# One root chain for both halves of a head slab and for two DeltaNet output tiles, and the identity kept inside the DeltaNet factor

## The chip, the core and the metric

The kernel runs on one core of a Trainium2 chip. Five engines work side by side on it: TensorE (PE, with its weight loads shown apart as PEld), VectorE (DVE), ScalarE (ACT), GpSimd (POOL) and SyncE (SP), which issues the DMAs. The metric is the device time of one execution in microseconds (us), and lower is better.

## The reference, cut to what matters

One layer of a decoder trunk on 512 tokens of width 1024. A normed input is projected once; its columns feed a gated DeltaNet (six heads of 64), a sparse attention (six query heads, two key/value heads) and a causal pooling. Their outputs are joined, projected back and added to the input, and a squared-ReLU MLP of width 4096 follows.

```python
def rms_norm(x, g):
    return xf * lax.rsqrt(jnp.mean(xf * xf, axis=-1, keepdims=True) + EPS) * g

# gated delta rule, chunks of 64 tokens
L = jnp.where(strict, einsum('bhncd,bhnsd->bhncs', k_beta, k) * decay, 0.0)
A = jnp.eye(C) + L
u = triangular_solve(A, v * beta, lower=True, unit_diagonal=True)
w = triangular_solve(A, k_beta * jnp.exp(gc), lower=True, unit_diagonal=True)
...
# DeltaNet output, per head
o = rms_norm(o, norm_g) * jax.nn.silu(z)
# attention: q, ks, kw are rms-normed per head of 64
q = rms_norm(q.reshape(B, T, NSA_HEADS, Dh), q_norm)
ks = rms_norm(ks, k_norm[1]); kw = rms_norm(kw, k_norm[2])
```

## The kernel before, in words

Tokens lie on the partitions in four tiles of 128 (`NT` = 4). The program runs in stages that flow into one another: input norm and first projections (to about 40 us), projection slabs for the DeltaNet with their convolutions (to about 120 us), the remaining slabs side by side with the DeltaNet solves and scan (to about 240 us), attention and output projection (to about 395 us), and the MLP (the rest).

**Order.** `side_by_side` (L935) merges five tracks into one program text: `solves`, `preps`, `slabs`, `compress` and `scans`. The context is opened with `schedule_with_timeline_sim=True`, so the order on each engine is fixed when the program is built, from the dependences and an estimate of durations; the program text sets priorities. At run time each engine works through its own list in that order.

**Root chain.** `rsqrt` (L101) finds a reciprocal root on DVE: a shift (L103), a multiply-add on the bits (L104) and three rounds of three small operations (L110, L111, L112). The caller puts one scaling ahead of it (L533 or L920) and sometimes one behind it (L536).

**Head slabs.** `prep_heads` (L521) norms the heads of one slab and transposes them. It is called three times: with four query heads that lie in `zt`, with a slab of two query and two key heads, and with a slab of two key heads; the latter two come out of `proj_tok` (L416), whose products lie in two PSUM banks `pss[0]` and `pss[1]`, one for token tiles 0 and 1, one for 2 and 3. For each half `b`: Square on ACT (L531, the first write of a buffer `qks`), sum on DVE (L532), scaling and root chain, product with the root (L537, the last read of `src[b]`), product with the norm weights on POOL (L540), then per tile a copy on ACT (L544, the first write of a buffer `X`) and a remainder on POOL (L545). The transposes (L549) and copies into `XT` (L552, L556, L557) follow when all four `X` are there. `qks`, `X`, `XT`, `Vt` and others share one pool of 27 buffers, `r2` (`t2`, L80). The banks of `pm` (L68) are 0, 1 and 2, so that of two successive slabs of `proj_tok` the second needs one bank of the first.

**DeltaNet.** `gdn_prep_k` (L747) makes the factor `LT` of a tile and its negative in fp16, `L16` (L767). `gdn_solve` (L812) builds an approximate inverse in fp16 and refines it with two calls of `residual` (L841): `IX` = I - `X` on DVE (L842), twelve-pair products of `LT` and `X` on PE (`sysmm`, L794), and `IX` minus them (L844). Four solves run, in two pairs side by side. `gdn_step` (L867) is the scan, nine steps long; its PSUM bank is number 3.

**DeltaNet output.** `gdn_out(i)` (L912) takes tile `i` when the scan has written it: Square (L918), sum (L919), scaling (L920) and root chain, product (L922), product with the gate on POOL (L923), three transposes into bank 3 (L926) and three pairs of copies out of it (`split_rows`, L147 to L149, into `yTh`, `yTl`). The four calls share bank 3 one after the other. Attention takes its accumulators from banks 7 and 3 (`pa`, L1054), so that its second head (`acc`, L1160) needs bank 3 after all four calls.

Of the kernel before, what the change touches and what calls it, by code (L numbers as in the profile page):

```python
# [9 lines left out]
F32 = mybir.dt.float32  # L10
# [27 lines left out]
def trunk_kernel(ctx, tc, x, norm_mix, w_in, conv_w, a_log, dt_bias, gdn_norm, nsa_q_norm, nsa_k_norm,  # L38
# [14 lines left out]
    def nm(s):  # L53
        _n[0] += 1
        return f"{s}{_n[0]}"
# [24 lines left out]
    def t2(shape, name, dt=F32):  # L80
        return r2.tile(shape, dt, tag="t", name=nm(name), bufs=N2)
# [19 lines left out]
    def rsqrt(y, a, n, p=P):  # L101

        V.tensor_single_scalar(y.bitcast(I32), a.bitcast(I32), 1, ALU.logical_shift_right)  # L103
        V.tensor_scalar(y.bitcast(I32), y.bitcast(I32), -1.0, float(0x5EF759DF - 0x80000000), ALU.mult, ALU.add)  # L104
        t = sml.tile([P, n], F32, tag=f"rs{n}", name=nm("rs"))[:p]
        for _ in range(3):
            if n == 1:
                V.scalar_tensor_tensor(t, y, a, y, ALU.mult, ALU.mult)
            else:
                V.tensor_tensor(t, y, y, ALU.mult)  # L110
                V.tensor_tensor(t, t, a, ALU.mult)  # L111
            V.scalar_tensor_tensor(y, t, -1.5, y, ALU.add, ALU.mult)  # L112
# [408 lines left out]
    def prep_heads(src, kg, qn, dst):  # L521


        n = len(dst)
        X = [t2([P, 4, P], "X") for _ in range(NT)]
        for b in range(2):
            scr = t2([P, 2, 4, HD], "qks")
            s_ = scr[:, :, 0:n]
            ss = sml.tile([P, 2, n], F32, tag=f"ssp{n}", name=nm("ss"))
            r = sml.tile([P, 2, n], F32, tag=f"rp{n}", name=nm("r"))  # L530
            S.activation(s_, src[b], AF.Square)  # L531
            V.tensor_reduce(ss, s_, AX.X, ALU.add)  # L532
            V.tensor_scalar(ss, ss, 0.5 / HD, 0.5 * EPS, ALU.mult, ALU.add)  # L533
            rsqrt(r.rearrange("p i h -> p (i h)"), ss.rearrange("p i h -> p (i h)"), 2 * n)
            if qn:
                V.tensor_scalar(r[:, :, 0:qn], r[:, :, 0:qn], 0.125, None, ALU.mult)  # L536
            V.tensor_tensor(s_, src[b], r.unsqueeze(3).to_broadcast([P, 2, n, HD]), ALU.mult)  # L537
            if qn < n:
                for i in range(2):
                    G.tensor_tensor(s_[:, i, qn:n], s_[:, i, qn:n],  # L540
                                    gk_b[:, kg].unsqueeze(1).to_broadcast([P, n - qn, HD]), ALU.mult)
            for i in range(2):
                x_ = X[2 * b + i]
                S.copy(x_[:, 0:n, 0:HD].bitcast(F32R), s_[:, i])  # L544
                G.tensor_tensor(x_[:, 0:n, HD:P], s_[:, i], x_[:, 0:n, 0:HD], ALU.subtract)  # L545
        for h, x0 in enumerate(dst):
            ps = pn()
            for i in range(NT):
                PE.transpose(ps[:, ts(i, P)], X[i][:, h, :], ident)  # L549
            XT[x0] = t2([P, T], "XT", F32R)  # L550
            if h < qn:
                S.copy(XT[x0], ps)  # L552
            else:
                XT[x0 + 1] = t2([P, T], "XT", F32R)
                for c in range(2):
                    S.copy(XT[x0 + c][halves[c]], ps[halves[c]])  # L556
                    V.tensor_copy(XT[x0 + c][halves[1 - c]], ps[halves[c]])  # L557
        return 0.43 * n
# [147 lines left out]
    gt = gte.enter_context(pool("gt", 1))  # L706
    GB = dict(kT=2, D1=2, LT=4, QK=4, qdT=4, tmp=3, gls=2, vn=2, S=3, L16=4)
    for a in range(2):
        GB.update({f"X{a}": 1, f"IX{a}": 1, f"TT1{a}": 1, f"T{a}": 4, f"R{a}": 2})

    def bch(r):
        return r.unsqueeze(2).to_broadcast([P, H, HD])

    def bs(m):
        return m.unsqueeze(1).to_broadcast([P, 6, 64])
# [31 lines left out]
    def gdn_prep_k(i):  # L747

        gU = w1t([P, 2, 3, 64], "gU", "tmp")
        gi = g[:, i].rearrange("p (j a) -> p a j", a=2)  # L750
        for hp in range(2):
            G.tensor_tensor(gU[:, hp], gi[:, hp].unsqueeze(2).to_broadcast([P, 3, 64]),
                            le64.unsqueeze(1).to_broadcast([P, 3, 64]), ALU.mult)
        de = pp_()
        PE.matmul(de[:, 0:384], sgt, gU.rearrange("p a j c -> p (a j c)"), start=True, stop=False, skip_group_check=True)
        PE.matmul(de[:, 0:384], identb, bs(nm64), start=False, stop=True, skip_group_check=True)
        yield 0.9
        D1, LT = w1t([P, 6, 64], "D1"), w1t([P, 6, 64], "LT")
        D0 = w1t([P, 6, 64], "D0", "tmp")
        S.activation(D1, v6(de), AF.Exp)  # L760
        V.tensor_tensor(D0, D1, bs(lt64), ALU.mult)
        kT = w1t([P, 3, 2, 64], "kT")
        S.copy(kT, head_T(kr[:, i]))
        yield 0.4
        yield from decayed(LT, kT, kT, D0)
        L16 = w1t([P, 6, 64], "L16", "L16", F16)
        V.tensor_scalar(L16, LT, -1.0, None, ALU.mult)  # L767
        grp[i] = dict(kT=kT, D1=D1, LT=LT, L16=L16)
        have.add(("k", i))

# [23 lines left out]
    def sysmm(pb, lhsT, rhs):  # L794

        ps = pb()
        for s_ in range(6):
            for p in range(2):
                PE.matmul(ps[halves[p], ts(s_, 64)], lhsT(halves[p], s_), rhs(halves[p], s_), start=True, stop=True)  # L799
        return v6(ps)  # L800

    def at(t):
        return lambda h, s_: t[h, s_]
# [8 lines left out]
    def gdn_solve(i):  # L812
# [7 lines left out]
        def tl(name, tag, dt=F32):  # L820
            return w1t([P, 6, 64], name, f"{tag}{ln}", dt)
# [14 lines left out]
                T16, TT16 = nt, tt  # L836
                yield 0.33

        X, IX = tl("X", "X"), tl("IX", "IX")

        def residual():  # L841
            V.tensor_tensor(IX, bs(id2), X, ALU.subtract)  # L842
            r = tl("R", "R", F16)
            V.tensor_tensor(r, IX, sysmm(pb, lambda h, s_: LT[h, s_], at(X)), ALU.subtract)  # L844
            return r

        G.tensor_copy(X, T16)
# [61 lines left out]
        yield 0.4  # L909
        return Sn  # L910

    def gdn_out(i):  # L912

        o = vb[:, i]
        sq = w1t([P, H, HD], "sq", "tmp")
        ss = sml.tile([P, H], F32, tag="ss6", name=nm("ss"))
        r = sml.tile([P, H], F32, tag="r6", name=nm("r"))
        S.activation(sq, o, AF.Square)  # L918
        V.tensor_reduce(ss, sq, AX.X, ALU.add)  # L919
        V.tensor_scalar(ss, ss, 0.5 / HD, 0.5 * EPS, ALU.mult, ALU.add)  # L920
        rsqrt(r, ss, 6)
        V.tensor_tensor(o, o, bch(r), ALU.mult)  # L922
        G.tensor_tensor(o, o, zt[:, i], ALU.mult)  # L923
        ps = go()
        for j in range(3):
            PE.transpose(ps[:, ts(j, P)], o[:, 2 * j:2 * j + 2].rearrange("p a d -> p (a d)"), ident)  # L926
        for j in range(3):
            split_rows(yTh[j][:, ts(i, P)], yTl[j][:, ts(i, P)], ps[:, ts(j, P)])


    def now(gen):
# [103 lines left out]
    slabs2 = late[-1]  # L1035
    flat = []
    side_by_side((90, solves()), (100, preps()), (102.0, slabs()), (10, compress()), (80, scans()))
    for i in range(NT):
        gdn_out(i)
    rgt0.close()  # L1040
    gte.close()
# [375 lines left out]
```

## Time and profile before

| what | value |
|---|---|
| median of 3 runs | 723.83 us (723.25 to 725.51) |
| the profiled execution | 724.29 us |
| its span | 722.50 us (1.79 us lie around it) |
| busy PE, DVE, ACT, POOL | 696.9, 554.8, 386.4, 170.6 us |
| granted TensorE clock | 0.995 of full speed |

A row of the timeline gives start and duration in us, engine, line, operation, output<-input, shape and count; what stands in brackets is the idle time of the engine just ahead of it and what ended that. A matmul's busy time runs to its modelled end, so successive matmuls overlap in it.

### The profile page before, as it was taken

What the parts mean: (1) busy time and instruction counts of PE and PEld (TensorE: products, weight loads), DVE (VectorE), ACT (ScalarE), POOL (GpSimd) and SP (SyncE); (2) the same over time, 40 slices, a digit from 0 to 9 for tenths busy, and PEclk for the clock granted to TensorE, in tenths of its full rate; (3) what the DMA queues carried; (4) which work ended last, traced back from release to release, by engine and by line L of the source; (5) the groups of instructions that cost most, each with busy time, mean ns of one, the idle gap of its engine ahead of it and who ended that gap; (6) DMA issues with size and microseconds to landing.
All of it is one profiled execution on the core that took longest, in us unless ns stands there. A gap on an engine that the chain in (4) does not pass through costs nothing.

```text
span 722.5 us, 13307 instructions
## 1 busy us (share of the span) xinstructions
PE 696.9 (96%) x5155; PEld 573.0 (79%) x5155; DVE 554.8 (77%) x1061; ACT 386.4 (53%) x768; POOL 170.6 (24%) x257
## 2 busy tenths in 40 slices
PE   8999999999999998999899999999999999999997
PEld 7888887888988776776579878888888888888885
DVE  5688998878686788877555997987968686886836
ACT  5455835565754558568633944444454544544430
POOL 5730004222123310000030330405032050504123
PEclk9999999999999999999999999999999999999999
DMA  6343223132410602222020153324051333311103
GB/s 222 92 108 102 73 60 88 32 96 61 129 31 4 234 1 59 88 88 89 1 87 2 59 176 117 116 84 131 20 174 59 121 112 117 117 55 65 56 0 116
DMA packets 49922, 62.20 MB, mean 86 GB/s; under 512 B 5494, under 2 KB 42564, under 8 KB 49860
## 3 DMA queue, kind: packets, MB, share of 16 engines
q1 hardware_dynamic: 48996, 61.16, 27.0%
q8 instruction: 40, 0.66, 0.4%
q10 hardware_dynamic: 864, 0.20, 0.1%
q14 instruction: 22, 0.18, 0.1%
HBM read 59.25 MB, written 2.10 MB: 85 GB/s over the span
## 4 chain that ended last, share of the span: by engine, by line
PE 71%; DVE 16%; ACT 4%; DMA 4%; issue 3%; POOL 1%; SPq 0%; DVEq 0%; ACTq 0%; POOLq 0%
PE ps L143 17%; PE ps L144 17%; PE ps L145 17%; PE ps L424 5%; PE ps L799 2%; PE ps L1139 2%; PE ps L1125 1%; DMA raw<-in_w_in_dram 1%; PE ps L587 1%; DVE lw L135 1%; DMA raw<-in_w_ffn_dram 1%; DMA x<-in_x_dram 1%; PE ps L1100 1%; DVE bl L1293 1%; DVE lwo L135 1%
## 5 line engine op out<-in xcount | busy, mean ns | idle before, releaser
L144 PE MATMUL ps<-h2l,hw 128*128 128x512 f32 (+1 forms) x280 | 105.1, 376 | 0.1
L145 PE MATMUL ps<-h2h,lw 128*128 128x512 f32 (+1 forms) x280 | 104.8, 375 | 0.0
L143 PE MATMUL ps<-h2h,hw 128*128 128x512 f32 (+1 forms) x280 | 104.0, 374 | 0.0
L1300 POOL TENSOR_TENSOR al<-gF,ah 128x512 fp32r<-128x512 f32 x24 | 36.2, 1508 | 225.4 <-ACT ah L1299 185.8
L143 PE MATMUL ps<-bh,ah 128*128 128x512 f32 x224 | 88.5, 395 | 0.7 <-DVE x L1386 0.7
L144 PE MATMUL ps<-bl,ah 128*128 128x512 f32 x224 | 88.1, 394 | 0.0
L145 PE MATMUL ps<-bh,al 128*128 128x512 f32 x224 | 84.6, 393 | 0.0
L1386 DVE TENSOR_TENSOR x<-ps,x 128x512 f32<-128x512 f32 x112 | 72.9, 681 | 10.6 <-PE ps L145 10.5
L1293 DVE TENSOR_TENSOR bl<-w2r,bh 128x1024 fp32r<-128x1024 f32 x40 | 57.8, 1447 | 6.8 <-ACT bh L1292 6.8
L144 PEld LDWEIGHTS ps<-h2l,hw 128*128 128x128 f32 x280 | 52.6, 188 | 10.4 <-DVE h2l L1264 0.3
L145 PEld LDWEIGHTS ps<-h2h,lw 128*128 128x128 f32 x280 | 52.6, 188 | 9.9
L143 PEld LDWEIGHTS ps<-h2h,hw 128*128 128x128 f32 x280 | 52.3, 188 | 10.2
L1300 POOL TENSOR_TENSOR al<-gS,ah 128x512 fp32r<-128x512 f32 x32 | 53.9, 1700 | 21.0 <-ACT ah L1299 21.0
L1292 ACT CAST bh<-w2r 128x1024 fp32r<-128x1024 f32 x40 | 41.8, 1047 | 28.9 <-PE ps L145 28.1
L135 DVE TENSOR_TENSOR lo<-raw,hi 128x512 fp32r<-128x512 f32 (+1 forms) x76 | 42.5, 582 | 13.8 <-ACT hi L134 11.2
L134 ACT CAST hi<-raw 128x512 fp32r<-128x512 f32 (+1 forms) x76 | 37.1, 519 | 28.6 <-DMA raw<-in_w_in_dram 7.6
L143 PEld LDWEIGHTS ps<-bh,ah 128*128 128x128 f32 x224 | 42.1, 188 | 11.4 <-ACT ah L1299 0.9
L145 PEld LDWEIGHTS ps<-bh,al 128*128 128x128 f32 x224 | 42.1, 188 | 9.7
L144 PEld LDWEIGHTS ps<-bl,ah 128*128 128x128 f32 x224 | 42.2, 188 | 9.5
L134 ACT CAST hw<-raw 128x1024 fp32r<-128x1024 f32 x32 | 32.1, 1046 | 26.2 <-PE ps L144 23.1
L135 DVE TENSOR_TENSOR lw<-raw,hw 128x1024 fp32r<-128x1024 f32 x32 | 40.1, 1287 | 5.3 <-ACT hw L134 5.3
L1299 ACT CAST ah<-gS 128x512 fp32r<-128x512 f32 x32 | 19.8, 621 | 45.1 <-DVE gS L1368 24.5
(373 smaller groups left out, 1703.0 us busy)
## 6 DMA issues: line engine op xcount, KB each, us to landing
raw<-in_w_ffn_dram SPq DMA_DIRECT2D x32, 512.0 KB, 3.9
w2r<-in_w_ffn_dram SPq DMA_DIRECT2D x32, 512.0 KB, 4.6
raw<-in_w_in_dram SPq DMA_DIRECT2D x24, 256.0 KB, 2.9
raw<-in_w_in_dram SPq DMA_DIRECT2D x36, 128.0 KB, 2.6
x<-in_x_dram SPq DMA_DIRECT2D x8, 512.0 KB, 6.6
raw<-in_cmp_w_dram SPq DMA_DIRECT2D x32, 128.0 KB, 2.6
raw<-in_w_out_dram SPq DMA_DIRECT2D x8, 512.0 KB, 4.0
out_dram<-x SPq DMA_DIRECT2D x8, 256.0 KB, 2.0
```

Of the source, the lines that this page charges most:

```text
L134: {"A": S.copy, "V": V.tensor_copy, "G": G.tensor_copy}[e[0]](hi[:, k], r)
L135: {"V": V, "G": G}[e[1]].tensor_tensor(lo[:, k], r, f32v(hi[:, k]), ALU.subtract)
L143: PE.matmul(ps, ah, bh, start=start, stop=False, **kw)
L144: PE.matmul(ps, ah, bl, start=False, stop=False, **kw)
L145: PE.matmul(ps, al, bh, start=False, stop=stop, **kw)
L424: PE.matmul(ps[:, ts(i, 256)], a_[:, k, ts(2 * b + i, P)], w_, start=(k == 0 and n_ == 0 and i == 0), stop=(k == KC - 1 and n_ == 2 and i ...
L799: PE.matmul(ps[halves[p], ts(s_, 64)], lhsT(halves[p], s_), rhs(halves[p], s_), start=True, stop=True)
L1292: S.copy(hi, src)
L1293: V.tensor_tensor(lo, src, f32v(hi), ALU.subtract)
L1299: S.copy(hi, src)
L1300: G.tensor_tensor(lo, src, f32v(hi), ALU.subtract)
L1386: V.tensor_tensor(x2[i][:, cs], acc[bk, t_], x2[i][:, cs], ALU.add)
```

## The change

Three edits.

1. `prep_heads`: both halves are squared and summed first, into one `ss` of twice the width; one scaling, one root chain and one optional scaling by 0.125 follow; then the products, POOL steps and copies of half 0 and half 1. The two `qks` buffers are asked for ahead of the chain.
2. `gdn_out` takes two tiles per call, `i0` and `i0 + 1`: two squares and sums, one scaling and root chain of width 12, then product, gate, transposes and copies of each tile. It is called for 0 and 2.
3. `gdn_prep_k` adds the identity to `LT` after `L16` is made, and `residual` subtracts the product of `LT` and `X` from the identity directly. The buffers `IX` go.

```diff
         n = len(dst)
         X = [t2([P, 4, P], "X") for _ in range(NT)]
+        ss = sml.tile([P, 2, 2, n], F32, tag=f"ssp{n}", name=nm("ss"))
+        r = sml.tile([P, 2, 2, n], F32, tag=f"rp{n}", name=nm("r"))
+        scr = [t2([P, 2, 4, HD], "qks")[:, :, 0:n] for _ in range(2)]
         for b in range(2):
-            scr = t2([P, 2, 4, HD], "qks")
-            s_ = scr[:, :, 0:n]
-            ss = sml.tile([P, 2, n], F32, tag=f"ssp{n}", name=nm("ss"))
-            r = sml.tile([P, 2, n], F32, tag=f"rp{n}", name=nm("r"))
-            S.activation(s_, src[b], AF.Square)
-            V.tensor_reduce(ss, s_, AX.X, ALU.add)
-            V.tensor_scalar(ss, ss, 0.5 / HD, 0.5 * EPS, ALU.mult, ALU.add)
-            rsqrt(r.rearrange("p i h -> p (i h)"), ss.rearrange("p i h -> p (i h)"), 2 * n)
-            if qn:
-                V.tensor_scalar(r[:, :, 0:qn], r[:, :, 0:qn], 0.125, None, ALU.mult)
-            V.tensor_tensor(s_, src[b], r.unsqueeze(3).to_broadcast([P, 2, n, HD]), ALU.mult)
+            S.activation(scr[b], src[b], AF.Square)
+            V.tensor_reduce(ss[:, b], scr[b], AX.X, ALU.add)
+        V.tensor_scalar(ss, ss, 0.5 / HD, 0.5 * EPS, ALU.mult, ALU.add)
+        rsqrt(r.rearrange("p b i h -> p (b i h)"), ss.rearrange("p b i h -> p (b i h)"), 4 * n)
+        if qn:
+            V.tensor_scalar(r[:, :, :, 0:qn], r[:, :, :, 0:qn], 0.125, None, ALU.mult)
+        for b in range(2):
+            s_ = scr[b]
+            V.tensor_tensor(s_, src[b], r[:, b].unsqueeze(3).to_broadcast([P, 2, n, HD]), ALU.mult)
...
         V.tensor_scalar(L16, LT, -1.0, None, ALU.mult)
+        V.tensor_tensor(LT, LT, bs(id2), ALU.add)
...
-            V.tensor_tensor(IX, bs(id2), X, ALU.subtract)
             r = tl("R", "R", F16)
-            V.tensor_tensor(r, IX, sysmm(pb, lambda h, s_: LT[h, s_], at(X)), ALU.subtract)
+            V.tensor_tensor(r, bs(id2), sysmm(pb, lambda h, s_: LT[h, s_], at(X)), ALU.subtract)
...
-    def gdn_out(i):
+    def gdn_out(i0):
...
+        for k in range(2):
+            sq = w1t([P, H, HD], "sq", "tmp")
+            S.activation(sq, vb[:, i0 + k], AF.Square)
+            V.tensor_reduce(ss[:, k], sq, AX.X, ALU.add)
         V.tensor_scalar(ss, ss, 0.5 / HD, 0.5 * EPS, ALU.mult, ALU.add)
-        rsqrt(r, ss, 6)
-        V.tensor_tensor(o, o, bch(r), ALU.mult)
-        G.tensor_tensor(o, o, zt[:, i], ALU.mult)
-        ps = go()
...
+        rsqrt(r.rearrange("p k h -> p (k h)"), ss.rearrange("p k h -> p (k h)"), 2 * H)
+        for k in range(2):
+            i = i0 + k
+            o = vb[:, i]
+            V.tensor_tensor(o, o, bch(r[:, k]), ALU.mult)
+            G.tensor_tensor(o, o, zt[:, i], ALU.mult)
+            ps = go()
...
-    for i in range(NT):
+    for i in (0, 2):
         gdn_out(i)
```

## Rows read from the trace of the kernel before

**Rows 1.** The page: busy time, share of the span, instructions.

```profile
PE 696.9 (96%) x5155; PEld 573.0 (79%) x5155; DVE 554.8 (77%) x1061; ACT 386.4 (53%) x768; POOL 170.6 (24%) x257
```

**Rows 2.** Stretches: span; busy us of PE, PEld, DVE, ACT, POOL; clock; DMA, GB/s.

```profile
87.00:104.00 17.00, 17.00 (x143) 13.46 (x142) 16.58 (x46) 7.87 (x21) 1.01 (x1) 1.00 0.19 47
120.00:240.00 120.00, 114.82 (x2058) 102.91 (x2058) 90.34 (x267) 69.96 (x180) 32.21 (x52) 1.00 0.21 58
154.00:171.60 17.60, 16.46 (x357) 14.33 (x355) 16.21 (x48) 10.57 (x28) 1.06 (x3) 1.00 0.38 114
199.00:206.60 7.60, 6.64 (x140) 6.00 (x138) 7.30 (x36) 5.25 (x17) 1.01 (x2) 1.00 0.02 4
240.00:308.00 68.00, 63.35 (x483) 47.68 (x480) 58.30 (x168) 44.04 (x114) 7.41 (x9) 0.97 0.29 101
...
395.00:722.50 327.50, 323.12 (x1423) 262.80 (x1421) 253.33 (x260) 154.20 (x204) 89.52 (x56) 1.00 0.29 94
```

**Rows 3.** Timeline of PE and DVE: slab products and the half's product ahead of them.

```profile
153.97 0.28 PE L424 MATMUL ps<-hi,hTl 128*128 128x256 f32 x1
...
170.28 0.69 DVE L537 TENSOR_TENSOR qks<-ps,r 128x512 f32<-128x512 f32 x1
...
171.59 0.39 PE L424 MATMUL ps<-hi,hTh 128*128 128x256 f32 x1
...
207.70 0.42 DVE L537 TENSOR_TENSOR qks<-ps,r 128x256 f32<-128x256 f32 x1
...
208.21 0.39 PE L424 MATMUL ps<-hi,hTh 128*128 128x256 f32 x1
```

**Rows 4.** Timeline of ACT: the first two calls of `prep_heads`.

```profile
133.08 0.63 ACT L531 ACTIVATE qks<-zt 128x512 f32<-128x512 f32 x1
...
142.11 0.63 ACT L531 ACTIVATE qks<-zt 128x512 f32<-128x512 f32 x1
...
149.57 0.71 ACT L544 CAST X<-qks 128x256 fp32r<-128x256 f32 x2 [2.54 <-DVE qks L537]
...
159.75 0.58 ACT L552 CAST XT<-ps 128x512 fp32r<-128x512 f32 x1
160.24 0.60 ACT L531 ACTIVATE qks<-ps 128x512 f32<-128x512 f32 x1
...
172.52 0.60 ACT L531 ACTIVATE qks<-ps 128x512 f32<-128x512 f32 x1
```

**Rows 5.** Timeline of DVE: a sum, and small operations of root chains.

```profile
136.52 0.17 DVE L111 TENSOR_TENSOR rs<-rs,ss 128x8 f32<-128x8 f32 x1
136.72 0.17 DVE L112 SCALAR_TENSOR_TENSOR r<-rs,r 128x8 f32<-128x8 f32 x1
...
173.16 0.69 DVE L532 TENSOR_REDUCE ss<-qks 128x8 f32<-128x512 f32 x1 [1.13 <-ACT qks L531]
...
174.71 0.17 DVE L111 TENSOR_TENSOR rs<-rs,ss 128x8 f32<-128x8 f32 x1
174.81 0.21 DVE L108 SCALAR_TENSOR_TENSOR rs<-r,ss 64x1 f32<-64x1 f32 x1
```

**Rows 6.** Groups by line and shape: `IX`.

```profile
L842 DVE TENSOR_TENSOR IX<-id,X 128x384 f32<-128x384 f32 x8 | 4.9, 608 | 0.0
```

**Rows 7.** Timeline of DVE: the first `L16`, and one of four `IX`.

```profile
93.05 0.35 DVE L767 TENSOR_SCALAR L<-LT 128x384 f16<-128x384 f32 x1
...
163.51 0.56 DVE L842 TENSOR_TENSOR IX<-id,X 128x384 f32<-128x384 f32 x1
```

**Rows 8.** Timeline of POOL and PE: the last DeltaNet output tiles, bank 3.

```profile
292.03 1.00 POOL L923 TENSOR_TENSOR vb<-vb,zt 128x384 f32<-128x384 f32 x1 [25.52 <-DVE vb L922]
...
294.59 0.52 PE L926 MATMUL ps<-ident,vb 128*128 128x128 f32 x3
...
300.52 0.49 PE L926 MATMUL ps<-ident,vb 128*128 128x128 f32 x3
...
307.42 0.64 PE L1160 MATMUL ps<-pcT,VCz 96*128 96x512 f32 x2
```

More of the change, by code (lines that the diff above doesn't have):

```diff
@@ L708, in trunk_kernel @@
     for a in range(2):
-        GB.update({f"X{a}": 1, f"IX{a}": 1, f"TT1{a}": 1, f"T{a}": 4, f"R{a}": 2})
+        GB.update({f"X{a}": 1, f"TT1{a}": 1, f"T{a}": 4, f"R{a}": 2})
     def bch(r):
@@ L837, in gdn_solve @@
                 yield 0.33
-        X, IX = tl("X", "X"), tl("IX", "IX")
+        X = tl("X", "X")
         def residual():
-            V.tensor_tensor(IX, bs(id2), X, ALU.subtract)
             r = tl("R", "R", F16)
-            V.tensor_tensor(r, IX, sysmm(pb, lambda h, s_: LT[h, s_], at(X)), ALU.subtract)
+            V.tensor_tensor(r, bs(id2), sysmm(pb, lambda h, s_: LT[h, s_], at(X)), ALU.subtract)
             return r
@@ L910, in gdn_step @@
         return Sn
-    def gdn_out(i):
[L914 to L919, printed above, removed]
-        V.tensor_scalar(ss, ss, 0.5 / HD, 0.5 * EPS, ALU.mult, ALU.add)
-        rsqrt(r, ss, 6)
-        V.tensor_tensor(o, o, bch(r), ALU.mult)
-        G.tensor_tensor(o, o, zt[:, i], ALU.mult)
-        ps = go()
[L925 to L928, printed above, removed]
+    def gdn_out(i0):
+        ss = sml.tile([P, 2, H], F32, tag="ss6", name=nm("ss"))
+        r = sml.tile([P, 2, H], F32, tag="r6", name=nm("r"))
+        for k in range(2):
+            sq = w1t([P, H, HD], "sq", "tmp")
+            S.activation(sq, vb[:, i0 + k], AF.Square)
+            V.tensor_reduce(ss[:, k], sq, AX.X, ALU.add)
+        V.tensor_scalar(ss, ss, 0.5 / HD, 0.5 * EPS, ALU.mult, ALU.add)
+        rsqrt(r.rearrange("p k h -> p (k h)"), ss.rearrange("p k h -> p (k h)"), 2 * H)
[5 more added lines that the diff above has]
+            ps = go()
+            for j in range(3):
+                PE.transpose(ps[:, ts(j, P)], o[:, 2 * j:2 * j + 2].rearrange("p a d -> p (a d)"), ident)
+            for j in range(3):
+                split_rows(yTh[j][:, ts(i, P)], yTl[j][:, ts(i, P)], ps[:, ts(j, P)])
     def now(gen):
```

## The prediction

> **What bounds the kernel now.** I read the page first, then the busy time by stretches, then the chain of waits, and last the timeline around the lines of the change. On the page PE looks like the bound [rows 1], but a matmul counts as busy to its modelled end, and one share is a mean over stages. By stretches: from 395 us on, the MLP keeps PE at 323.12 of 327.50 us, and nothing of this change lies there. Whatever is gained or lost ahead moves that block as a whole. From 120 to 240 us DVE is busy 90.34 of 120 us, and it is nearly full just where the chain of waits leaves PE: 16.21 of 17.60 us from 154 to 171.6, 7.30 of 7.60 us from 199 to 206.6 [rows 2]. There a DVE operation less is worth something. In attention (240 to 308) DVE has 58.30 of 68 us; 87 to 104 is full as well (16.58 of 17) [rows 2].
>
> The timeline tells what PE lacks there. The last slab product before the hole ends at 154.25; the next starts at 171.59, right after the product of the first half with its root (170.28 + 0.69 = 170.97) has read its PSUM bank for the last time. At 207.70 + 0.42 = 208.12 the same: the next slab product starts at 208.21 [rows 3]. So I read these holes as slab products waiting for a bank that `prep_heads` holds. The pace of `prep_heads` sets the pace of the slabs.
>
> That pace is serial. In call 1 the second Square starts at 142.11, 9 us after the first (133.08), though its input is in SBUF long before; in call 2 it is 172.52 after 160.24; and call 2's first Square comes straight after call 1's last `XT` copy (159.75 + 0.58) [rows 4]. I infer, and no row proves it, that buffers of the shared pool are given out in the order of first writes: the second `qks` behind the first two `X`, the next call behind the last `XT`.
>
> **The change, part by part.** I sum against the profiled execution, 724.29 us (span 722.50 and 1.79 around it); it lies 0.46 above the median 723.83.
>
> *Small operations.* Two of three calls lose 13 (scaling, 2 + 9 of the root, the 0.125), the third 12; `gdn_out` loses two chains of 12: 62 in all. Alone in a chain two follow each other by 136.72 - 136.52 = 0.20 us; between others by 174.81 - 174.71 = 0.10 [rows 5]. That is 6.2 to 12.4 us of DVE, but it counts only in full stretches. Wider operands I cost at nothing: 8 to 16 columns are small beside either figure, and there are few operations left to widen.
>
> The Trainium skill ("VectorE: DVE Perf Modes", section "The DRAIN you can't avoid") says the next operation does not start until the pipe has emptied. By that each removed one would free its whole 0.17 us, the terms at 0.10 below would be 0.9 and 0.8 us larger, and the sum -5.3. The 0.10 between starts at 0.17 duration does not agree [rows 5], and the rows decide.
>
> *prep_heads call 1.* The second half's `X` copies come at 149.57, the first half's right before 142.11 [rows 4]. One chain saves the distance, about 8 us, less what now stands ahead of the first half's copies: Square 0.63, sum 0.69, product 0.69 and 0.7 of copies [rows 3 to 5], together 2.7. So call 1 ends up to 5.4 us earlier, and the Square of call 2 can move from 160.24 to 154.9.
>
> *prep_heads call 2.* From the first Square to the end of its product it takes 170.97 - 160.24 = 10.7 us. The second Square and sum come into it (0.60 + 0.69 = 1.3); four `IX` leave the stretch, each 0.55 long and worth a step of some 0.47, since neighbours in a full queue overlap a little (174.71 + 0.17 reaches 0.07 beyond 174.81) = 1.9. So the bank comes free 5.4 + 0.6 = 6.0 us earlier at best. At worst the calls keep their place and only the 1.3 against 1.9 stands: 0.6. DVE is 92% full there [rows 2], and its other work does not vanish but follows later, as does the work PE fills the hole with; I take the middle, **-3.3**. The second chain of call 2 (13 operations, 0.10 each, from 173.16 on, in step with a chain of `compress` that PE waits for) is gone: **-1.0** (0 to -1.9).
>
> *199 to 206.6.* The chain of output tile 0 leaves (12 at 0.10, and a product 0.5 that moves to where tile 1 is done): -1.7. The Square and the sum of call 3's second half come ahead of the product that frees the bank; at its own 0.42 each [rows 3] that is +0.8. Net -0.9, bounds -1.7 and +0.8; with PE behind it at once, I take **-0.9**.
>
> *IX.* Eight go, 4.9 us [rows 6]. Four are counted above [rows 7]; the other four belong to the second pair of solves and lie beside the products of `sysmm`, which don't wait for `IX`: nothing. Without that cover one step of 0.47 would come, so -0.5 at best.
>
> *Identity into LT.* Four additions of 128x384, as long as an `IX` (0.55). The solve starts from `L16`, so no one waits for the sum itself; what is queued behind it on DVE does. The first two stand behind `L16` at 93.05 [rows 7], where DVE is full and slab products wait for it: 2 x 0.47 = **+0.9**. The second two, of tiles 2 and 3, have their solve far behind them and lie beside slab products: +0.2 (0 to +0.9).
>
> *gdn_out.* Tiles 0 and 1 have to be ready when the scan gives bank 3 free, and lie in the scan's first half: nothing, and if their joint chain were later than that, one 0.20 step for each operation still open. Tile 2 loses its own early chain and waits for tile 3's sum. Before, tile 3's chain and gate end at 293.03 and the transposes of tile 2 start at 294.59 [rows 8]. With one more product of 0.55 and tile 2's gate of 1.00 in line, tile 2 is ready at about 293.6 and tile 3 at 294.6, still ahead of 294.59 and 300.52. Some slip is likely: **+0.5** (-1.0 to +5.9; the upper end is a rival below).
>
> **Sum:** -3.3 - 1.0 - 0.9 + 0.9 + 0.2 + 0.5 = -3.6. So 724.29 - 3.6 = 720.7, and on the median's scale 723.83 - 3.6 = **720.2 us**.
>
> **The rivals.**
>
> *More of it arrives (715.8).* If the calls of `prep_heads` really close up, all of 6.0 us comes, with 1.9 and 1.7: -9.6, plus 1.1 for the identity and 0.5 for the tail, -8.0 and 723.83 - 8.0 = 715.8. For it: the start of slab products within 0.7 us of the bank's release, twice [rows 3]. Against it: the solves and the scan run beside the slabs, and attention's second head waits for the scan.
>
> *Hidden anyway (723.5).* The scan, not the slabs, sets when bank 3 comes free, and attention's second head starts only at 307.42 [rows 8]. If the slabs' lead dies there, of the sum only -0.9 - 0.5 + 1.1 = -0.3 remains, and PE waits in other places for the same end.
>
> *PE full after all (723.8).* From 120 to 240 the weight loads alone keep PE's load side busy for 102.91 of 120 us, more than DVE's 90.34 [rows 2]. If that is the bound, a lighter DVE brings nothing there. The Trainium skill ("Perfetto Trace Analysis", section "Identifying the Most-Contended Engine") would have TensorE judged so, and the most contended engine mended first. Against it: in the MLP, where PE is never idle for long, the same figure is only 262.80 of 327.50, 80% against 86%, so small loads that run side by side must fill it; and the two holes end at a product of DVE [rows 3].
>
> *Slower (728.7).* Tile 2 of the DeltaNet output now hangs on tile 3's sum. If the joint chain is ready more than 1 us later than before, the transposes of tile 2 are late; if it slips to where tile 3's stood, by 300.52 - 294.59 = 5.9 us, bank 3 and attention's second head come as much later. The order on DVE sets that: from 240 to 308 it is 86% full [rows 2], and the chain's operations stand between longer ones. With the slabs' lead lost in that wait and only call 2's second chain kept: 723.83 + 5.9 - 1.0 = 728.7.
>
> That the change doesn't do what it says is no rival here: the operations are removed in the text. But the order on each engine is laid out anew, so that a step may move for no reason named here.
>
> **How the numbers follow.** Forecast (717.5 to 721.5): 0.42. More arrives (below 717.5): 0.18. Hidden: 0.18; PE full: 0.04; both between 721.5 and 726. Slower: 0.18. 0.3% is 2.2 us, about what a measurement can tell from no change, so 721.6 to 726.0 is "same". Faster is 0.42 + 0.18 = 0.60, same 0.18 + 0.04 = 0.22, slower 0.18. The range leaves out the outer part of the two end cases: 713.5 to 727.5.
>
> **What would show it.** Right: both Squares of a `prep_heads` call next to each other; the slab products resume before 170 and the hole is shorter; DVE less busy in all by some 6.2 to 12.4 us and 4.9 - 2.2 = 2.7 for `IX` and the identity; the second head's first accumulation ahead of 304. The identity's price: the next slab products after 95 us start later by up to 1 us. Wrong: a hole as long as before with another release at its end; or the transposes of tile 2 waiting for POOL's gate, with the second head after 308. If the slabs end earlier and attention's end does not move, the lead died at bank 3.

## The result, and the profile after

The changed kernel takes 735.22 us (733.12 to 735.44) against 724.26 us (723.25 to 725.51) for the kernel before on the same chip: a ratio of 1.013, 95% interval 1.010 to 1.016. The forecast was 720.2. The profiled execution took 733.12 us, its span 731.1 against 722.5, so 8.6 us more.

DVE's busy time fell by only 2.6 us, from 554.8 [rows 1], though 66 of its operations are gone. The page of the changed kernel:

```profile
PE 700.8 (96%) x5155; PEld 575.8 (79%) x5155; DVE 552.2 (76%) x995; ACT 386.0 (53%) x768; POOL 173.0 (24%) x257
```

What was forecast for the slabs came. Timeline of DVE and PE, changed kernel:

```profile
164.08 1.29 DVE L538 TENSOR_TENSOR qks<-ps,r 128x512 f32<-128x512 f32 x2
...
164.82 0.39 PE L424 MATMUL ps<-hi,hTh 128*128 128x256 f32 x1 [1.14 <-DVE qks L538]
```

Both halves' products now stand together. The slab products resume at 164.82 instead of 171.59 [rows 3], and the row names the product with the root as what ended the wait. The last slab product comes at 234.3 instead of 238.7.

But the end moved the other way. One row for each line, with its first and last start; first the kernel before: the copy of a solve's last product (`ke`, L864) and the scan's copies of its output (L908).

```profile
L864 ACT ACTIVATE kr<-ps x4: 484/490/512, 167.5 to 233.9; 128x384 f32<-128x384 f32 x4
...
L908 ACT COPY vb<-ps x16: 311/313/317, 176.8 to 277.1; 64x192 f32<-64x192 f32 x16
```

The same two lines of the changed kernel:

```profile
L865 ACT ACTIVATE kr<-ps x4: 474/486/490, 180.4 to 243.3; 128x384 f32<-128x384 f32 x4
...
L909 ACT COPY vb<-ps x16: 312/313/315, 190.7 to 284.2; 64x192 f32<-64x192 f32 x16
```

And attention's second head in its timeline, which was at 307.42 [rows 8]:

```profile
314.31 0.63 PE L1164 MATMUL ps<-pcT,VCz 96*128 96x512 f32 x2
```

The first solve ends 12.9 us late, the last 9.4, the scan 7.1, the second head 6.9, and the whole span 8.6. The first pair's masked copies up to 138 us are at most 1.6 us late. So most of the loss arises between 140 and 180 us, in the first pair of solves, and is carried to the end.

### The profile page after: what moved, and what is told of

Its sections match the earlier page's. It is cut to its first block, busy times and chain, and to the rows that moved or that the text cites. A ratio compares the mean times of both kernels' runs of the same rounds, so it can differ in the third digit from the quotient of the medians.

```text
span 731.1 us, 13234 instructions
## 1 busy us (share of the span) xinstructions
PE 700.8 (96%) x5155; PEld 575.8 (79%) x5155; DVE 552.2 (76%) x995; ACT 386.0 (53%) x768; POOL 173.0 (24%) x257
## 4 chain that ended last, share of the span: by engine, by line
PE 73%; DVE 14%; ACT 4%; DMA 4%; issue 3%; POOL 2%; SPq 0%; DVEq 0%; ACTq 0%; POOLq 0%
PE ps L143 18%; PE ps L144 18%; PE ps L145 18%; PE ps L424 4%; PE ps L801 2%; DMA raw<-in_w_ffn_dram 2%; PE ps L1143 2%; PE ps L1129 1%; DVE lw L135 1%; PE ps L588 1%; DMA x<-in_x_dram 1%; PE ps L905 1%; DVE bl L1297 1%; PE ps L1104 1%; DVE lwo L135 1%
## 5 line engine op out<-in xcount | busy, mean ns | idle before, releaser
L135 DVE TENSOR_TENSOR lo<-raw,hi 128x512 fp32r<-128x512 f32 (+1 forms) x76 | 44.6, 611 | 14.5 <-ACT hi L134 12.2
L135 DVE TENSOR_TENSOR lw<-raw,hw 128x1024 fp32r<-128x1024 f32 x32 | 40.1, 1287 | 9.9 <-ACT hw L134 9.8
```

Of the source, the lines that this page charges most:

```text
L135: {"V": V, "G": G}[e[1]].tensor_tensor(lo[:, k], r, f32v(hi[:, k]), ALU.subtract)
```

## The experiments

Theories, as they are named in the expectations. **F**: the DeltaNet chain (first pair of solves, second pair, nine steps of the scan, then attention's second head) sets the end; delays in it are carried, a lead of the slabs is not. **A**: the slab products set free early stand on PE ahead of the solves. **B**: the identity delays the solves. **C**: each edit has the order of instructions laid out anew, and that costs by itself. **D**: the joint output chain is late.

Each ratio is against the kernel before on the same chip. The kernel before differs by up to 1.4 us from chip to chip, so the differences below are taken against its median on the same chip.

| run | median us | before | ratio (95%) |
|---|---|---|---|
| prep_only | 731.04 | 724.12 | 1.009 (1.006 to 1.012) |
| id_only | 736.63 | 724.12 | 1.017 (1.013 to 1.020) |
| out_only | 725.74 | 724.38 | 1.002 (1.001 to 1.004) |
| no_prep | 740.36 | 724.12 | 1.022 (1.019 to 1.025) |
| id_late | 738.45 | 725.11 | 1.019 (1.017 to 1.020) |
| id_pool | 728.32 | 725.11 | 1.005 (1.004 to 1.007) |
| id_after | 731.43 | 724.38 | 1.010 (1.008 to 1.012) |
| after_pool | 729.62 | 724.38 | 1.008 (1.005 to 1.011) |
| after_hold | 739.36 | 724.12 | 1.020 (1.016 to 1.023) |
| prep_hold | 739.78 | 725.52 | 1.020 (1.017 to 1.023) |
| prep_c1 | 735.27 | 725.52 | 1.013 (1.011 to 1.016) |
| prep_c2 | 732.10 | 725.52 | 1.010 (1.007 to 1.013) |
| prep_c3 | 732.03 | 725.52 | 1.009 (1.006 to 1.012) |
| nudge2 | 731.63 | 724.51 | 1.011 (1.008 to 1.013) |
| nudge4 | 731.47 | 724.51 | 1.009 (1.007 to 1.012) |
| scan2 | 717.85 | 725.11 | 0.991 (0.989 to 0.992) |
| after_scan2 | 725.90 | 725.11 | 1.001 (1.000 to 1.003) |
| scan2_go | 718.31 | 724.38 | 0.991 (0.990 to 0.993) |

### Each part alone

**prep_only**: the joint root chain in `prep_heads` alone. 

> The kernel before with one part of the change: the joint root chain of both halves in prep_heads. Theory A (the slab products that the joint chain sets free stand on PE ahead of the first pair of DeltaNet solves, whose chain of small products sets the end): nearly the whole loss comes with this part, 730 to 736 us; the last step of the first pair's second solve ends near 180 us of the records instead of 168.6, and the first slab product after the hole comes near 165 us instead of 171.6. Rival B (the identity's additions and the lost IX delay the solves): 720 to 724, first pair ends at 169 or earlier. Rival D (the joint output chain is late): 720 to 724, too.

**out_only**: the joint output chain in `gdn_out` alone. 

> The kernel before with the joint output chain of two tiles alone. Theory F (the DeltaNet chain sets the end and only what delays it counts): the scan ends within 2 us of 277.1, the transposes of output tiles 2 and 3 come within 2 us of 294.6 and 300.5, 722 to 727. The slower rival of the prediction (tile 2 hangs on tile 3's sum): the transposes of tile 2 come near 300 and the time is 727 to 731.

**id_only**: the identity in `LT` alone. 

> The kernel before with the identity added to LT and IX gone, nothing else. Theory A: 722.5 to 725.5, first pair of solves within 1.5 us of 168.6. Rival B: most of the 11 us, 730 to 735. Rival C (any edit moves the order laid out by some us either way): a change of more than 3 us with no delay of the solves at the residuals.

**no_prep**: the identity and the joint output chain together. 

> The changed kernel with prep_heads as before (one chain for each half), so the identity in LT and the joint output chains alone. Theory A: 722 to 726, the first pair of solves ends within 2 us of 168.6 and the hole in the slab products from 154 to 171 is back. Rival B: 730 to 735. Rival D: 727 to 730 with the first pair of solves in its place and only the tail (transposes of output tiles 2 and 3) late.

Measured against before: +6.9, +1.4, +12.5 and +16.2 us. The joint output chain costs next to nothing: its transposes of tiles 2 and 3 came 3 us late (297.6 and 303.4), more than the 2 us expected, but about half of what the slower rival of the prediction needed. D falls, and that rival with it. The identity, held for the cheapest part, costs most; id_only lies above B's range, and no_prep above every range that was named for it.

The joint root chain costs too, within A's range, but not in A's way. In prep_only the first slab product behind the hole comes no earlier than before:

```profile
172.15 0.39 PE L424 MATMUL ps<-hi,hTh 128*128 128x256 f32 x1 [0.49 <-DVE qks L538]
```

A expected it near 165; the kernel before had 171.59 [rows 3]. All the same the first pair ends at 176.2 instead of 168.6, its fifth masked copy comes at 143.6 instead of 140.4, and the windows show a granted clock of 0.91 from 160 to 180. So slab products that are set free early are not what this part alone costs. The parts don't add up, either: 6.9 + 1.4 + 12.5 = 20.8, and all three together cost 11.0.

### Where the identity's price is

In **id_only** the four additions take the place of eight `IX`. Its DVE timeline at the fourth one:

```profile
138.07 0.36 DVE L767 TENSOR_SCALAR L<-LT 128x384 f16<-128x384 f32 x1
...
138.46 1.22 DVE L768 TENSOR_TENSOR LT<-LT,id 128x384 f32<-128x384 f32 x1
139.61 1.18 DVE L825 COPY_PREDICATED W<-lv,L 128x384 f16<-128x384 uint16 x1
140.71 0.79 DVE L536 TENSOR_SCALAR r<-r 128x8 f32<-128x8 f32 x1
141.54 0.69 DVE L537 TENSOR_TENSOR qks<-zt,r 128x512 f32<-128x512 f32 x1
142.15 0.55 DVE L829 CAST_PREDICATED W<-lv,ps 128x384 f16<-128x384 uint16 x1
```

The kernel before at the same place:

```profile
138.47 0.36 DVE L767 TENSOR_SCALAR L<-LT 128x384 f16<-128x384 f32 x1
...
138.86 0.56 DVE L824 COPY_PREDICATED W<-lv,L 128x384 f16<-128x384 uint16 x1
139.34 0.17 DVE L536 TENSOR_SCALAR r<-r 128x8 f32<-128x8 f32 x1
139.53 0.69 DVE L537 TENSOR_TENSOR qks<-zt,r 128x512 f32<-128x512 f32 x1
140.37 0.56 DVE L828 CAST_PREDICATED W<-lv,ps 128x384 f16<-128x384 uint16 x1
```

Tile 3's own solve is far off, but the first pair's fifth masked copy (L828, now L829) stands a few places behind on the same engine. From `L16` to that copy it took 1.90 us; now it takes 4.08. The addition is 1.22 long instead of 0.55, and the next two are stretched as well, beside POOL's products (id_only):

```profile
138.44 0.83 POOL L791 TENSOR_TENSOR qr<-kr,egc 128x384 f32<-128x384 f32 x1 [5.66 <-PE ps L733]
139.23 1.15 POOL L779 TENSOR_TENSOR qd<-qr,egc 128x384 f32<-128x384 f32 x1
140.34 1.14 POOL L792 TENSOR_TENSOR kr<-kr,egc 128x384 f32<-128x384 f32 x1
```

The two engines take turns: POOL's products stretch from 0.83 to 1.15, and the addition and the masked copy behind it (L825), which have two inputs in SBUF, to 1.22 and 1.18. The Trainium skill ("SBUF — State Buffer", section "Who interferes with whom") has this as a rule: a DVE instruction with two inputs in SBUF and a GpSimd instruction that reads SBUF exclude each other. The trace agrees, 1.22 against 0.55. The third one (L536, 0.79) has one input in SBUF and a constant, so the rule as told here does not cover it. The masked copy that reads a PSUM bank kept 0.56 beside such a product in the kernel before (140.37 above):

```profile
139.84 1.07 POOL L790 TENSOR_TENSOR qr<-kr,egc 128x384 f32<-128x384 f32 x1 [7.39 <-PE ps L733]
```

PE waits for that copy, and then its clock falls for a while. Timeline of PE, id_only:

```profile
140.33 0.59 PE L742 MATMUL ps<-qT,kT 64*64 64x64 f32 x18
142.75 0.38 PE L800 MATMUL ps<-W,TT 64*64 64x64 f16 x12 [1.83 <-DVE W L829]
...
143.28 0.28 PE L424 MATMUL ps<-hi,hTl 128*128 128x256 f32 x1
143.39 0.30 PE L424 MATMUL ps<-hi,hTh 128*128 128x256 f32 x1
143.51 0.40 PE L424 MATMUL ps<-lo,hTh 128*128 128x256 f32 x1
143.71 0.42 PE L424 MATMUL ps<-hi,hTl 128*128 128x256 f32 x1
143.92 0.41 PE L424 MATMUL ps<-hi,hTh 128*128 128x256 f32 x1
```

The same products that started 0.12 us apart start 0.21 apart from 143.51 on, which is the lower of the two levels, 1.2 instead of 2.4 GHz. The windows from 140 to 200 us, in steps of 20, show a granted clock of 0.91, 0.86 and 0.89; the kernel before had 1.00 in all three. Only the 0.91 lies behind this pause. The other two come from a second stretch that is three times as long; finer windows show it in their last column but two:

```profile
143.60:146.80 3.20, 3.20 (x22) 2.91 (x21) 3.06 (x10) 2.31 (x5) 1.53 (x3) 0.50 0.03 5
147.00:174.00 27.00, 24.78 (x443) 20.96 (x442) 18.49 (x57) 16.16 (x41) 5.87 (x9) 1.00 0.34 94
174.30:184.40 10.10, 9.09 (x96) 8.06 (x96) 6.91 (x30) 3.19 (x11) 2.79 (x5) 0.50 0.09 22
```

So three quarters of what the clock costs here come some 30 us behind the copy. PE pauses 0.72 and 0.37 us just ahead of that stretch, for remainders of `X` on POOL; that the late copy leads to it is not shown. The changed kernel keeps 1.00 there and loses it later, 0.81 and 0.94 from 280 to 320 against 0.91 and 1.00.

**id_late** moves the additions in the text, into each solve ahead of the first residual. 

> The identity alone, with the additions still on VectorE but moved into each solve, behind its last squaring step and ahead of the first residual, where the four IX used to begin. Theory F: nothing stands ahead of the masked copy at 140.4 any more, the additions fall near 153 to 157 beside work of ACT; 721 to 727. Rival C: 732 to 738.

 It took 738.45, far outside F's range, and its trace has the additions at 95.3, 107.9, 133.9 and 139.7: the layout puts an operation where its data are ready, and the order on PE is the same as in id_only, product for product. Moving a line of text moved nothing.

**id_pool** and **id_after** do move them.

```diff
-        V.tensor_tensor(LT, LT, bs(id2), ALU.add)      # id_only, in gdn_prep_k
+        G.tensor_tensor(LT, LT, bs(id2), ALU.add)      # id_pool
...
+            mc = V.copy_predicated(W, bs(lv[:, m]), yp)      # id_after, in gdn_solve
+        with tc.issue_after(mc.ins):
+            V.tensor_tensor(LT, LT, bs(id2), ALU.add)
```

> The identity alone on the kernel before, as in the run with only that part, but with the four additions on GpSimd instead of VectorE. Theory F (the DeltaNet chain sets the end: first pair of solves, second pair, nine steps of the scan, then attention's second head; a delay in it is carried to the end): the addition of tile 3 at 138.5 us, 1.22 long, stood with two more slow operations ahead of the first solve's masked copy, PE idled 1.8 us and its clock fell. With the addition off VectorE that copy is back near 140.4, the clock is 1.00 from 140 to 200, and the time 722 to 727. Rival C (any edit makes the order laid out worse by as much): 732 to 738.

> The identity alone on VectorE, each addition held by an order edge behind the last masked copy of its own solve (the run that moved it only in the text left it where the data were ready, at 95, 108, 134 and 139.7). Theory F: the fifth masked copy is back at 140 to 141.5, PE's clock is 1.00 from 140 to 200, the first pair ends within 2 us of 168.6, 721 to 728. Rival C: 732 to 739.

Measured 728.32 and 731.43, that is +3.2 and +7.1 where id_only had +12.5: 9.3 and 5.5 us come back. As expected, the fifth masked copy is back (141.7 and 140.9), the clock is 1.00 from 140 to 200, and the first pair ends at 168.6 in both. The second pair even ends 3 to 4 us earlier than before (`ke` at 230.0 and 230.6 instead of 233.9). Yet both stay 3.2 and 7.1 us above the kernel before, outside what F allowed: the scan's last five steps take longer, and the last copy comes at 280.3 and 279.3. The lower clock, too, is not gone but comes later: from 200 to 220 and from 240 to 260 us the windows show 0.83 in id_pool and 0.91 in id_after, against 1.00 in the kernel before.

**after_pool** is the changed kernel with the additions on GpSimd. 

> The changed kernel with the four additions of the identity on GpSimd instead of VectorE. Theory F: of the delay of the first pair's solves a part goes (the fifth masked copy from 144.5 to about 143), while the joint chain's operations on VectorE and the earlier slab products on PE stay ahead of the residuals: 727 to 734. If the addition's place were all of it: 720 to 726. If it does nothing in this order: 734 to 737.

 It took 729.62, 5.6 less than the changed kernel and inside F's range, but the sign that F named did not come: the fifth masked copy stays at 144.8. DVE's timeline of the changed kernel:

```profile
140.03 1.22 DVE L769 TENSOR_TENSOR LT<-LT,id 128x384 f32<-128x384 f32 x1
...
143.31 1.29 DVE L538 TENSOR_TENSOR qks<-zt,r 128x512 f32<-128x512 f32 x2
144.52 0.55 DVE L830 CAST_PREDICATED W<-lv,ps 128x384 f16<-128x384 uint16 x1
```

And of after_pool:

```profile
142.36 2.51 DVE L538 TENSOR_TENSOR qks<-zt,r 128x512 f32<-128x512 f32 x2
144.79 0.55 DVE L830 CAST_PREDICATED W<-lv,ps 128x384 f16<-128x384 uint16 x1
```

The addition is gone from the queue, but the two products of the joint chain, which now stand together ahead of the copy, are stretched beside POOL and take its place. In this order the copy is held by the joint chain too, and what the 5.6 us came from is not shown; the first pair ends at 174.4 instead of 180.7.

### What the joint root chain does

In the changed kernel, other than in prep_only, the slab products that come early stand on PE in the tail of the first solves. Timeline of PE; L801 are products of a solve:

```profile
167.09 0.28 PE L424 MATMUL ps<-hi,hTh 128*128 128x256 f32 x1
167.29 0.38 PE L801 MATMUL ps<-R,TT 64*64 64x64 f16 x12
...
171.66 0.28 PE L424 MATMUL ps<-hi,hTl 128*128 128x256 f32 x1
171.87 0.37 PE L801 MATMUL ps<-TT,R 64*64 64x64 f16 x12
172.08 0.89 PE L801 MATMUL ps<-X,LT 64*64 64x64 f32 x24
```

Slab products run without a hole from 164.82 to 167.09, and again ahead of 171.87, each time with a solve's product next in the list. The hole of [rows 3] was no idle time: the first pair's residuals ran in it, and PE was busy 16.46 of its 17.60 us [rows 2].

**after_hold** and **prep_hold** put the hole back, on the changed kernel and on prep_only: each product of the slab behind call 2 gets an edge of order behind the first pair's last product.

```diff
+        with (tc.issue_after(after().ins) if after else ExitStack()):
             PE.matmul(ps[:, ts(i, 256)], a_[:, k, ts(2 * b + i, P)], w_,
```

> The changed kernel with one more rule of order: the products of the slab that follows prep_heads' second call stand on PE behind the last product of the first pair of solves. Nothing else is edited. Theory A: the hole that the solves ran in is back, the first pair ends near 171 instead of 180.7 (not 168.6, for the joint chains still stand before its steps on DVE), and the time falls to 722 to 728. If the solves are late for what stands on DVE alone (rival E: joint chains and the additions ahead of their steps), the first pair still ends after 176 and the time stays at 732 to 736.

> The joint chain in all three calls, with the products of the slab behind call 2 held on PE behind the first pair of solves (as was done on the changed kernel). Theory F with one bound more (PE has the slab products to do anyway, and what is held back stands beside the scan later): the first pair ends within 3 us of 168.6, but the slabs end after 240 and the scan's last five steps take longer than the 43 us of before; 726 to 734. If the slab products' place ahead of the residuals is the whole loss: 720 to 726.

The first pair came back as A and F said: 170.4 instead of 180.7, and 171.3 instead of 176.2. The time did not, and lies outside every range that was named: 739.36 and 739.78, which against the kernel before on the same chip is 4 and 7 us more than without the edge. Two things show why. The slab products have to be done anyway and now stand beside the scan, whose last copy comes at 287.7 and 289.6. And PE, with nothing to fill the waits of the solves, falls to the lower clock; the window of prep_hold:

```profile
160.00:180.00 20.00, 17.16 (x225) 14.31 (x225) 12.83 (x41) 7.98 (x23) 5.18 (x8) 0.61 0.19 57
```

So in the changed kernel A names a true delay, but not a loss that can be had back by holding the products.

**prep_c1**, **prep_c2**, **prep_c3**: one of the three calls joint, the others as before.

> The kernel before with the joint chain in prep_heads' first call alone (the two other calls with a chain for each half). Theory F: the joint chain and both products stand on VectorE ahead of the fifth masked copy (140.4 before, 143.6 with the joint chain in all three calls), and call 2 may start earlier, so slab products come earlier into the tail of the first pair of solves: most of the loss of the run with all three calls, 728 to 733, first pair ends after 174. If the loss comes from call 2: 722 to 726.

> The joint chain in the second call alone. Call 2 keeps its start (first Square near 160), both products come near 171, the slab products resume at 171 to 173: the first pair of solves stays within 2 us of 168.6. Theory F: 722 to 727. If the joint chain of call 2 on VectorE is what delays the residuals: 728 to 733 with the first pair after 171.

> The joint chain in the third call alone, near 206 to 215 us, beside the second pair of solves. Theory F: no operation of the first pair is touched; 721 to 727. If the joint chain delays the second pair on VectorE as it did the first: 727 to 731 with the second pair's ke after 236.

735.27, 732.10 and 732.03. Call 1 moves the first pair as expected (the fifth masked copy at 142.9, the last end at 174.9), though by more time than expected; the other two should have cost nothing by F, and cost 6.6 and 6.5. prep_c2 met both signs of its rival (728 to 733, the first pair after 171: it ends at 171.9, where nudge2, below, has 169.4), so call 2's chain does delay the solves. prep_c3 leaves everything up to 206 us in its place and takes work away.

**nudge2** and **nudge4** test whether any edit at these places costs as much: the kernel before with one operation of 0.17 us more, a multiplication of the first half's sums by 1.0, in call 2 or in call 3.

```diff
+            if kg == 1 and b == 0:      # nudge4: kg == 2
+                V.tensor_scalar(ss, ss, 1.0, None, ALU.mult)
             rsqrt(r.rearrange("p i h -> p (i h)"), ss.rearrange("p i h -> p (i h)"), 2 * n)
```

> The kernel before with one operation more: in prep_heads' second call the first half's sums are multiplied by 1.0 once (128x8, 0.17 us on VectorE near 164 us). Nothing is joined and no identity moved. If only the work and its place count (theory F without rival C): 724 to 726. If the order that is laid out anew behind any edit in this stretch costs by itself (rival C): 728 to 736, with the scan's last output copy 3 us or more behind 277.1.

> The same single operation in prep_heads' third call (near 207 us), the place at which the run with the joint third call alone lost 6.5 us though its work got less. Theory F without C: 724 to 726. Rival C: 728 to 735, from the same point of the order on (the second pair's last steps and the scan).

+7.1 and +7.0 us, for 0.17 us of work. C holds. PE's list of products is that of the kernel before up to 170.3 us in nudge2 and up to 208.2 in nudge4, and another one behind that. Beside these prices (+7.1 and +7.0), the joint calls' +6.6 in call 2 and +6.5 in call 3 say nothing against the joining itself. Call 1 and the places of the identity have no such control, so how much of their +9.8 and +12.5, or of the change's +11.0, is the new order stays open. What the price is made of can be seen ahead of attention's second head; timeline of PE, nudge4:

```profile
306.63 0.72 PE L145 MATMUL ps<-hwo,yTl 128*128 128x512 f32 x2
310.03 0.79 PE L143 MATMUL ps<-hwo,yTh 128*128 128x512 f32 x1 [2.67 <-ACT yTh L148]
310.62 0.63 PE L144 MATMUL ps<-lwo,yTh 128*128 128x512 f32 x1
311.05 0.63 PE L143 MATMUL ps<-hwo,yTh 128*128 128x512 f32 x1
...
316.39 0.40 PE L1162 MATMUL ps<-pcT,VCz 96*128 96x512 f32 x1
```

A product of the output projection stands in PE's list 2.67 us before its input is there. Everything behind it waits, then runs at the lower clock (311.05 - 310.62 = 0.43 us apart; in the kernel before the same pair of lines is 306.95 - 306.72 = 0.23 apart), and the second head starts 12 us after the last output transposes (304.3), where the kernel before needed 6.9 [rows 8]. The changed kernel has such a pause itself, a weight's remainder from DVE being late:

```profile
298.48 0.50 PE L144 MATMUL ps<-lwo,yTh 128*128 128x512 f32 x1 [2.41 <-DVE lwo L135]
```

Pauses of PE of over 0.8 us between 100 and 330 us add up, in the modelled ends of the trace, to 3.0 us in the kernel before, 2.1 in scan2, 4.6 in out_only, 6.6 in the changed kernel, 6.1 in id_only and 8.7 in nudge4; the order of the sums is not quite that of the times (prep_c2: 3.3), so the sum describes, it does not explain all.

### Is the DeltaNet chain the bound

**scan2** lets steps 5 and 7 of the scan use the bank of the second solve lane, which is free by then; **after_scan2** does so in the changed kernel.

```diff
-        ps = ps_()
+        ps = (pgb if t in (5, 7) else ps_)()
```

> The kernel before with one edit: steps 5 and 7 of the scan take the PSUM bank of the second solve lane, which is free by then, instead of bank 3, so that a step's first products need not wait for the copy of the output of the step ahead. Theory F: from its state (234.1) to the next step's copy (240.8) the scan waits for bank 3; with two banks the last output copy comes at 255 to 270 instead of 277.1, attention's second head at 293 to 303 instead of 307.4, and the time is 712 to 720. If the slab products set the end, as predicted, or PE is simply full: 722 to 726.

> The changed kernel with the same second bank for steps 5 and 7 of the scan. Theory F: as the loss of the change lies in the same chain, shortening its last part gives as much here as in the kernel before, 720 to 729, still some 8 to 11 above the kernel before with that edit. If the loss lay behind the scan (in attention's own order), it would stay at 733 to 736.

DVE's timeline of the kernel before, from a step's state to the next step's copy:

```profile
234.08 0.36 DVE L899 TENSOR_TENSOR S<-ps,gls 128x192 f32<-128x192 f32 x1 [1.34 <-PE ps L896]
...
240.81 0.35 DVE L887 COPY vn<-ps 128x192 f32<-128x192 f32 x1
```

And with the second bank:

```profile
235.47 0.36 DVE L899 TENSOR_TENSOR S<-ps,gls 128x192 f32<-128x192 f32 x1 [1.34 <-PE ps L896]
239.61 0.36 DVE L887 COPY vn<-ps 128x192 f32<-128x192 f32 x1 [3.77 <-PE ps L883]
```

6.7 us become 4.1. The scan's last copy comes at 264.2 instead of 277.1, the second head at 301.68, and the time falls by 7.3 us to 717.85; the changed kernel comes to 725.90, +0.8 where it had +11.0. Nothing of the slabs is touched, and PE's list is that of the kernel before up to 236.5 us, so F holds as far as the scan: the end hangs on this chain. This order, too, is laid out anew behind that point, and 7 us is what a neutral operation moves; what speaks for the chain is that the step got shorter, that the scan ended where F said, and that both kernels gain. This version beats both kernels. Of the gap of 11.0 between the two, 8.1 us stay, as F expected of a loss that arises ahead of the scan.

**scan2_go** also puts the output transposes into that bank (`go = banks(5)`). 

> The kernel before with the second bank for the scan's steps 5 and 7, and the transposes of the DeltaNet output in that same bank instead of bank 3. If attention's second head waits for bank 3 to the last output transpose (295.5 with the second bank alone, the head's accumulation at 301.7), its accumulation comes at 283 to 295 and the time is 705 to 715. If it waits for something else by now: 716 to 720.

 The second head came at 266.5, 35 us earlier than with the second bank alone, and the time stayed at 718.31: the fourth head starts at 308.0 instead of 313.5, and the last two end where they did (345.3 and 353.4 us). By then something other than bank 3 decides; what, was not tried. So the last link of F, attention's second head, is not shown to set the end; the scan is, with the reserve above.

## Why the prediction was wrong

*The bound.* Here it failed first. The holes between slab products were read as PE's loss, though PE was busy 16.46 of 17.60 us in the first [rows 2]. The wait was read rightly: the slab products resumed 171.59 - 164.82 = 6.8 us earlier, right behind the product with the root (though the joint chain alone, in prep_only, brought no lead: 172.15). But the pace of the slabs did not set the end. The sums -3.3, -1.0 and -0.9 were leads of work that the end does not wait for; the last slab product did come 4.4 us earlier, and none of it arrived. The rival "hidden anyway" had this, with the scan named as what decides, at a chance of 0.18 and with too small a consequence: it let the lead die and did not ask whom the earlier products push aside.

*The joint chain on DVE.* The sum asked how early the chain's end frees the bank, and had no term for what the chain and its two products, now side by side, stand ahead of. They stand ahead of the first pair's masked copies: with the joint chain alone the fifth comes at 143.6 instead of 140.4, and the first pair ends 7.6 us late (prep_only), 6.3 with call 1 alone.

*The identity.* "+0.2 (0 to +0.9)" for tiles 2 and 3 was the written term that came out farthest off. The step asked who waits for the sum and found no one; it should have listed what is queued behind the addition on DVE, where it would have found the first pair's masked copy; it did so for the first two additions, at +0.9, and not for these. In id_only the copy came 1.8 us late, and the run lost 12.5. And 0.55 was the duration beside an idle POOL, not the 1.22 beside its products. With its place corrected, id_only still costs 3 to 7 us.

*IX, second pair: nothing.* Open: the second pair ends 3 to 4 us earlier where the place of the additions is mended (id_pool, id_after). Whether the missing `IX` or the new order does that, these runs don't tell.

*gdn_out, +0.5.* Right: +1.4 alone, with an interval from 0.7 to 2.5. The rival that made it the slower case was the wrong one.

*Small operations.* The term of -1.0 for call 2's second chain is not worked out: 13 at 0.10 are 1.3, which would have made the forecast 719.9, and its bound of -1.9 has no source. 62 did go, and DVE's two bounds for them were 6.2 to 12.4 us, with 2.7 more for `IX`. Busy time fell by 2.6: the four additions took 3.37 instead of 2.2, and the remainders of the weights (L135) took 3.0 more.

*The order laid out anew.* The prediction noted that a step may move for no reason named, and gave that neither price nor chance. Two runs put it at 7 us, twice the largest term of the sum. Each difference was summed as if the other instructions kept the order of before, while 0.17 us more on DVE costs 7 us. With such a term, of unknown sign from the trace alone, the range of 713.5 to 727.5 was too narrow. The price is not one number: of the orders seen here without the second bank, out_only, which differs from before only behind some 200 us, came out 1.4 us above it, all others 3 to 16. Why the order of before is the better one, beyond the pauses shown, stays open.

## What to carry to other kernels

Ahead of costing an edit, look for the chain that the end hangs on by shortening it, and not by looking for holes alone: a hole in one stream of work on PE is where another stream runs, and filling it delays that one. Where the order is laid out by a planner, time the kernel before with one neutral operation at the same place, and compare the edit with that; a difference smaller than what this moves says nothing of the edit itself. An operation "off the path" is priced by what stands behind it on its engine, and at its duration beside the work it will meet there.

## What was unexpected of the hardware

In id_only a pause of PE of 1.83 us amid dense work was followed, 0.8 us after its end, by a stretch at the lower clock, in which 256-column products start 0.21 us apart instead of 0.12 (granted 0.91 over those 20 us, so 0.09 x 20 = 1.8 us of full speed lost, as much as the pause itself). DVE operations that have all operands in SBUF can be stretched by POOL's products even when tiny: a 128x8 scaling took 0.79 instead of 0.17.
